# Replanning the order of a threshold-attention kernel: planned scatter and split distances, and new draws

## The chip, the cores and the metric

One core of one Trainium2 chip runs the kernel. The engines are PE (matmuls), DVE, ACT and POOL (element-wise work), and SP, which here only issues DMAs. The metric is the device time of one execution in microseconds (us); smaller is better.

## What is computed

Attention over 96 heads (batch 8, 12 heads, 512 rows, 64 columns), in which only weights above a threshold of 0.1 are kept and then normalised again:

```
scores  = einsum('bhqd,bhkd->bhqk', Q, K) / sqrt(64)
weights = exp(scores - max);  weights /= sum(weights) + 1e-10
weights = where(weights > 0.1, weights, 0)
weights /= sum(weights) + 1e-10
out     = einsum('bhqk,bhkd->bhqd', weights, V)
```

With these random inputs few rows have a weight above 0.1. A row that has none is zero in the output, and a row with exactly one has that key's V row as its output.

## The kernel before

**The idea.** The kernel writes zeros over the whole output, finds the rows that can have a weight above the threshold with cheap arithmetic, recomputes those few rows exactly, fetches the V row of the key that was found, and scatters it into the output. A dense path behind a check at the end is there for inputs with many such rows; it isn't taken here.

**The work.** Two heads make a pair (48 pairs, `hp`), four heads a quad (24 quads, `hq`), eight heads a group (12 groups, `j`, 0 to 11).

For each quad the *main run* does the following. SP loads K (`k_sb`), POOL loads Q as 16-bit floats (`q_sb`, L221). PE transposes K (`ktr`, L333), ACT or DVE copies it out (`kt`, L317 or L319), and POOL casts each pair's half to 16 bits (`kf`, L321). POOL or DVE reorders Q (`qm`, L321 or L319), PE transposes it (`qtr`, L370), and DVE or ACT copies it out (`qt`). For each pair PE then makes four blocks of scores (`qk`, L386), ACT or DVE takes an exponential of each (`exp`, L394 or L396, a 128x1024 block each), PE sums and compares each block's keys with 32 matmuls a pair (`d`, L405), and DVE reduces that to one number a row (`dred`, L413).

For each group, eight units of work after its last exponentials (`LAG`), a chain of small steps follows:

- `flags` (L417, POOL or DVE) marks the rows that may exceed the threshold; `size` and `rank` (L429, L435, L437, PE) check sizes and number the flagged rows; `key` (L441, DVE) and `oh` (L445, DVE) turn the numbers into a one-hot; `idx` (L456, PE), `half` and `idxev` (L466, DVE) make the row indices.
- `gather` (L471, POOL) is an indirect DMA that fetches the flagged rows of Q; `split` (L479, POOL or DVE) puts them into `qb`; `xtr` (L486, PE), `xev` (copy to `xq`), `xqk` (L500, PE) and `xexp` (L507, ACT) recompute their scores and weights exactly.
- `tv` (L513, POOL or DVE) and `found` (L518, DVE) find the key above the threshold; `vidx` (L525) makes its index; `fetch` (L536, POOL) is an indirect DMA that fetches the V row into `vsel`, which `vzero` (L532, POOL) has cleared; `scatter` (L542, POOL) is an indirect DMA that writes it to the output.

**What sets the order.** A planner in the kernel's Python (`Schedule`) lays the steps out before anything is built. Each step is added with the engines it may run on and for each a pair of numbers, (occupancy, latency): the engine is taken for the first, and whoever depends on the step may start when the second is over. A step also has the steps it depends on, a due place (`prio`), and the buffers it takes and gives back. The planner always takes the step that can start first, and among those within 0.06 the one with the smallest due place. `DRAWS` is a list of seeds: each moves a random share of the due places (2, 10 or 40 per cent) by up to 2.5 either way, one draw on top of the other. So every number in the planner acts on the whole order and on the choice between engines.

The steps are then emitted in the planned order, and `keep` ties each instruction behind the one that was emitted before it on its engine. Two kinds of instruction can still move when the program is built. K loads and zero writes on SP aren't kept. And an indirect DMA emits a register move of its own (the trace shows it on POOL's queue at L471, L536 and L542); `keep` ties the DMA to that move, and the move to nothing. So a gather, fetch or scatter can stand earlier in the built program than in the plan, while the steps that were emitted behind it stay behind it.

POOL executes in order: while a scatter at the head waits for its V rows, the steps behind it (kf, qm, flags, tv) wait too.

Of the kernel before, what the change touches and what calls it, by code (L numbers as in the profile page):

```python
# [11 lines left out]
class Schedule:  # L12
# [10 lines left out]
    def add(self, name, engs, deps, prio, fn, takes=(), gives=()):  # L23
        self.ids[name] = len(self.ops)
        self.ops.append((name, engs, list(deps), prio, fn, list(takes), list(gives)))

    def order(self, draws=()):

        ops, ids = self.ops, self.ids
        shift = [0.0] * len(ops)  # L30
        for draw in draws:
            rng = random.Random(draw)
            share = (0.02, 0.1, 0.4)[draw % 3]
            for i in range(len(ops)):
                if rng.random() < share:
                    shift[i] += rng.uniform(-2.5, 2.5)
        n = len(ops)
        succ = [[] for _ in range(n)]
        need = [0] * n
        ready_at = [0.0] * n  # L40
        for i, op in enumerate(ops):
            for d in op[2]:
                succ[ids[d]].append(i)
                need[i] += 1
        free_at = {}
        taken = {p: [] for p in self.bufs}
        given = {p: {} for p in self.bufs}
        users = {}
        for op in ops:
            for at in op[6]:  # L50
                users.setdefault(at, [0, 0.0])[0] += 1
        ready = {}

        def offer(i):
            for eng in ops[i][1]:
                ready.setdefault(eng, []).append(i)

        for i in range(n):
            if need[i] == 0:
                offer(i)  # L60
        out = []

        def start(i, eng):
            t = max(ready_at[i], free_at.get(eng, 0.0))
            want = {}
            for pool, _ in ops[i][5]:
                k = len(taken[pool]) + want.get(pool, 0)
                want[pool] = want.get(pool, 0) + 1
                if k >= self.bufs[pool]:
                    at = k - self.bufs[pool]  # L70
                    rel = given[pool].get(taken[pool][at]) if at < len(taken[pool]) else None
                    if rel is None:
                        return None
                    t = max(t, rel)
            return t

        while len(out) < n:
            best = None
            for eng, lst in ready.items():
                ts = [(start(i, eng), i) for i in lst]  # L80
                ts = [(t, i) for t, i in ts if t is not None]
                if not ts:
                    continue
                t0 = min(t for t, _ in ts)
                prio, t, i = min((ops[i][3] + shift[i], t, i) for t, i in ts if t <= t0 + 0.06)
                if best is None or (t, prio) < best[:2]:
                    best = (t, prio, i, eng)
            assert best is not None, "the schedule is stuck"
            t, _, i, eng = best
            name, engs, deps, prio, fn, takes, gives = ops[i]  # L90
            occ, lat = engs[eng]
            for other in engs:
                ready[other].remove(i)
            out.append((t, i, eng))
            free_at[eng] = t + occ
            for pool, key in takes:
                taken[pool].append(key)
            for pool, key in gives:
                left = users[pool, key]
                left[0] -= 1  # L100
                left[1] = max(left[1], t + lat)
                if left[0] == 0:
                    given[pool][key] = left[1]
            for j in succ[i]:
                ready_at[j] = max(ready_at[j], t + lat)
                need[j] -= 1
                if need[j] == 0:
                    offer(j)
        self.timeline = sorted(out)
        self.taken = taken  # L110
        self.makespan = max(t + ops[i][1][eng][1] for t, i, eng in out)
        return [(ops[i][4], eng) for t, i, eng in self.timeline]
# [3 lines left out]
def kernel(  # L116
# [68 lines left out]


    LAG, WARM = 8.0, 7
    DRAWS = (67013, 12429, 32834, 12225, 15210, 2031, 21369, 91932)

    consts = ctx.enter_context(tc.tile_pool(name="consts", bufs=1))  # L190
    kload = ctx.enter_context(tc.tile_pool(name="kload", bufs=6))
# [24 lines left out]
    def load_q(hq, parts=1):  # L216
# [15 lines left out]
        out=identity_f32[:], in_=identity_f32[:],  # L232
# [6 lines left out]
        out=group_f[:], in_=group_f[:], compare_op=ALU.is_ge, fill=-1.0,  # L239
# [3 lines left out]
        out=group_f[:], in_=group_f[:], compare_op=ALU.is_ge, fill=-1.0,  # L243
# [176 lines left out]
    def do_size(j, n, eng):  # L420
        if n == 0:
            rk = mpsum.tile([P, 3 * KEY], f32, name="sm", tag="sm")
            T["rk", j] = rk
        rk = T["rk", j]
        for which in range(2):
            sq = T["kq"[which] + "sq", 2 * j + n // 2]
            for r in range(R):
                at = (1 + which) * KEY + n * C2 + 2 * r
                keep(nc.tensor.matmul(rk[:, at:at + 2], lhsT=sq[:, n % 2, r * P:(r + 1) * P], rhs=heads[:],  # L429
                                      start=True, stop=True))  # L430
# [122 lines left out]
    def do_check(part, eng):  # L553
        if part == 0:
            keep(nc.vector.tensor_scalar(ok_all[:], keys[:], SLOTS + 0.5, None, op0=ALU.is_le))
            keep(nc.vector.tensor_reduce(ok_one[:, 0:1], ok_all[:], axis=AX.XY, op=ALU.min))
        else:
            okk = small.tile([P, NO], f32)
            keep(nc.vector.tensor_scalar(okk[:], kept[:], -20000.0, None, op0=ALU.is_ge))
            keep(nc.vector.tensor_reduce(ok_one[:, 1:2], okk[:], axis=AX.X, op=ALU.min))  # L560
            keep(nc.vector.tensor_reduce(oks[:], ok_one[:], axis=AX.X, op=ALU.min))
# [12 lines left out]
    for hq in range(NQ):  # L574
        u0 = 8 * hq
        j = hq // 2
# [62 lines left out]
        last = j == NO - 1  # L639

        def stage(name, engs, deps, fn, takes=(), gives=(), j=j, x=x):
            add((name, j), engs, deps, x, lambda e: fn(j, e), takes=takes, gives=gives)

        stage("flags", {"POOL": (0.25, 0.4), "DVE": (0.12, 0.3)}, [("dred", 4 * j + n) for n in range(4)] + ["casts"], do_flags)
        for n in range(4):
            add(("size", j, n), {"PE": (0.2, 0.23)},
                [("ksq", 2 * j + n // 2), ("qsq", 2 * j + n // 2)] + ([("flags", j)] if n == 0 else [("size", j, n - 1)]), x,
                lambda e, j=j, n=n: do_size(j, n, e), takes=[("sm", ("rk", j))] if n == 0 else [],
# [4 lines left out]
        stage("idx", {"PE": (0.5, 0.78)}, [("oh", j)], do_idx, takes=[("sm", ("ix", j))])  # L653
        stage("half", {"DVE": (0.08, 0.24), "ACT": (0.2, 0.36)}, [("idx", j)], do_half)
        stage("idxev", {"DVE": (0.13, 0.30)}, [("half", j)], do_idxev, gives=[("sm", ("ix", j))])
        stage("gather", {"POOL": (1.1, 4.2 if last else 5.5)}, [("idxev", j)], do_gather)
        stage("split", {"POOL": (0.4, 0.55), "DVE": (0.21, 0.37)}, [("gather", j), ("half", j)], do_split)
        stage("xtr", {"PE": (0.12, 0.42)}, [("split", j)], do_xtr, takes=[("sm", ("xp", j))])
        stage("xev", {"DVE": (0.2, 0.35), "ACT": (0.2, 0.36)}, [("xtr", j)], do_xev, gives=[("sm", ("xp", j))])
# [4 lines left out]
        stage("found", {"DVE": (0.80, 1.0)}, [("tv", j)], do_found)  # L664
        stage("vidx", {"POOL": (0.22, 0.36), "DVE": (0.12, 0.28)}, [("found", j)], do_vidx)
        stage("vzero", {"POOL": (0.12, 0.25)}, [("gather", j)], do_vzero)
        stage("fetch", {"POOL": (1.1, 4.2 if last else 7.0)}, [("vidx", j), ("vzero", j)], do_fetch)
        stage("scatter", {"POOL": (1.1, 3.0)}, [("fetch", j), ("z", 2 * j), ("z", 2 * j + 1)], do_scatter)
        if last:
            stage("check0", {"DVE": (1.0, 1.2)}, [("key", j)], lambda j, e: do_check(0, e))  # L670
            stage("check1", {"DVE": (0.4, 0.6)}, [("found", j), ("check0", j)], lambda j, e: do_check(1, e))
    for step, eng in sched.order(DRAWS):
        step(eng)
# [105 lines left out]
```

## Time and profile before

| what | us |
|---|---|
| median of 3 runs (lowest to highest) | 245.99 (245.85 to 246.08) |
| the profiled execution | 244.09 |
| its span, from first to last instruction | 242.4 |
| busy: PE, DVE, ACT, POOL | 201.0, 182.4, 159.3, 130.7 |
| scatters' waits on POOL for V rows (L542) | 20.5 in 10 waits |
| splits' waits on POOL for gathered Q rows (L479) | 3.1 in 2 waits |

The first three rows are three views of one thing: the span is what the trace covers, the profiled execution's time holds what lies around it, and the median is of executions without a profile. Busy times count an engine's instructions; an engine can be idle because it waits for another, and the waits by engine name whom. The granted clock is the share of its full speed that PE was allowed in a stretch of time. "Landing" is the time from a DMA's issue until its data is there: a median of 3.1 us for the gathers, 3.6 for the fetches.

### The profile page before, as it was taken

Reading aid. Unit: us, or ns where it says so; the run is one execution under the profiler, and the core shown is the slowest. Engines: PE = TensorE matmul, PEld = TensorE weight load, DVE = VectorE, ACT = ScalarE, POOL = GpSimd, SP = SyncE. Lnnn points to the kernel's source line nnn. Section 1 sums busy time; section 2 is a strip of 40 time slices with the busy share of each in tenths; the row PEclk is TensorE's granted clock in tenths of the full one; section 3 lists DMA queues with packets and bytes.
Section 4 is the critical chain, followed back from the end, with each engine's and each line's share of the span. In section 5 each row is a group of like instructions: output and inputs, shape, how many; then the busy total and the mean of one; then the engine's idle time right before and its main releaser. Section 6 shows DMA issues by size and latency. Waiting matters only on the chain.

```text
span 242.4 us, 7238 instructions
## 1 busy us (share of the span) xinstructions
PE 201.0 (83%) x2997; PEld 128.3 (53%) x2997; DVE 182.4 (75%) x313; ACT 159.3 (66%) x190; POOL 130.7 (54%) x214
## 2 busy tenths in 40 slices
PE   6596999999699499999699998999995978993510
PEld 2274567666456247766456766666754455672000
DVE  5669779989597388999668899989796587795220
ACT  2466698988478187899559869898785576860110
POOL 5528055376444766567746857728666228233441
PEclk9779799999979679999979999999998599996555
DMA  7999989999999957464752685555540000000000
GB/s 135 209 228 344 212 290 292 288 275 257 348 342 251 250 87 136 63 110 99 137 88 51 118 130 88 92 117 111 70 94 9 0 3 8 3 8 5 2 6 14
DMA packets 68021, 32.55 MB, mean 134 GB/s; under 512 B 52278, under 2 KB 64708, under 8 KB 67985
## 3 DMA queue, kind: packets, MB, share of 16 engines
q1 hardware_dynamic: 53088, 24.91, 37.9%
q0 software_dynamic: 13840, 6.88, 21.9%
q8 instruction: 24, 0.39, 0.7%
q10 hardware_dynamic: 1056, 0.26, 0.5%
q14 instruction: 13, 0.10, 0.1%
HBM read 25.95 MB, written 12.98 MB: 161 GB/s over the span
## 4 chain that ended last, share of the span: by engine, by line
PE 51%; POOL 14%; issue 11%; DVE 11%; DMA 6%; ACT 5%; POOLq 0%; ACTq 0%; DVEq 0%
PE sc L386 16%; PE sm L405 14%; PE sc L333 8%; DVE e L396 5%; PE sm L500 4%; DMA vsel<-in_V_dram,vidx 4%; PE smh L370 3%; POOL kf L321 3%; POOL qsel L471 3%; PE sm L429 3%; ACT e L394 3%; POOL out_dram L542 2%; DMA k_sb<-in_K_dram 2%; POOL qm L321 2%; PE sm L456 2%
## 5 line engine op out<-in xcount | busy, mean ns | idle before, releaser
L394 ACT ACTIVATE e<-sc 128x1024 bf16<-128x1024 f32 x130 | 128.0, 1024 | 39.7 <-PE sc L386 38.3
L386 PE MATMUL sc<-qt,kf 64*128 64x512 f16 x384 | 69.8, 406 | 13.4 <-POOL kf L321 7.2
L396 DVE TENSOR_SCALAR e<-sc 128x1024 int16<-128x1024 f32 x62 | 75.0, 1219 | 7.6 <-PE sc L386 7.2
L405 PEld LDWEIGHTS <-e 128*128 128x128 bf16 x1536 | 54.5, 101 | 24.8 <-issue 23.9
L405 PE MATMUL sm<-groups,e 128*128 128x64 bf16 x1536 | 63.8, 198 | 0.6 <-DVE idx L466 0.4
L321 POOL CAST kf<-kt 128x512 f16<-128x512 f32 x46 | 28.9, 644 | 35.9 <-DVE kt L319 16.9
L413 DVE TENSOR_REDUCE stat<-sm 128x8 f32<-128x512 f32 x48 | 32.8, 685 | 10.9 <-PE sm L405 10.6
L386 PEld LDWEIGHTS <-kf 64*128 64x128 f16 x384 | 17.5, 95 | 32.1 <-issue 16.6
L333 PE MATMUL sc<-identity_f,k_sb 128*128 128x128 f32 x192 | 31.9, 297 | 1.5 <-DMA k_sb<-in_K_dram 1.5
L321 POOL COPY qm<-q_sb 128x512 f16<-128x512 f16 x43 | 26.6, 634 | 1.8 <-DMA q_sb<-in_Q_dram 1.7
L333 PEld LDWEIGHTS sc<-identity_f,k_sb 128*128 128x128 f32 x192 | 22.2, 150 | 9.0 <-issue 4.2
L542 POOL DMA_INDIRECT out_dram<-vsel,idx x12 | 12.5, 1038 | 20.8 <-DMA vsel<-in_V_dram,vidx 20.5
L221 POOL DMA_DIRECT2D q_sb<-in_Q_dram x25 | 20.4, 815 | 4.6 <-POOL qm L321 1.5
L370 PE MATMUL smh<-identity_h,qm 128*128 128x128 f16 x192 | 16.1, 229 | 4.7 <-POOL qm L321 2.8
L319 DVE COPY kt<-sc 128x1024 f32<-128x1024 f32 (+1 forms) x13 | 15.3, 1179 | 5.8 <-PE sc L333 5.7
L507 ACT ACTIVATE xe<-sm 128x512 f32<-128x512 f32 x12 | 7.2, 597 | 19.0 <-PE sm L500 18.9
L317 ACT COPY kt<-sc 128x1024 f32<-128x1024 f32 (+1 forms) x12 | 11.7, 979 | 8.7 <-DVE kt L319 4.6
L471 POOL DMA_INDIRECT qsel<-in_Q_dram,idx x12 | 12.9, 1076 | 8.4 <-DVE idx L466 5.9
L370 PEld LDWEIGHTS <-qm 128*128 128x128 f16 x192 | 12.0, 101 | 9.7 <-issue 4.6
L536 POOL DMA_INDIRECT vsel<-in_V_dram,vidx x12 | 13.5, 1122 | 5.2 <-POOL vidx L525 3.3
L500 PE MATMUL sm<-kt,xq 128*32 128x512 f32 x96 | 15.6, 726 | 0.6 <-DVE xq L319 0.5
L353 DVE TENSOR_SCALAR ksq<-kf 128x1024 int16<-128x1024 int16 x24 | 11.4, 475 | 4.8 <-POOL kf L321 4.8
(84 smaller groups left out, 176.1 us busy)
## 6 DMA issues: line engine op xcount, KB each, us to landing
out_dram<-zero SPq DMA_DIRECT2D x24, 512.0 KB, 6.2
k_sb<-in_K_dram SPq DMA_DIRECT2D x94, 128.0 KB, 4.3
q_sb<-in_Q_dram POOLq DMA_DIRECT2D x23, 256.0 KB, 5.0
k_sb<-in_K_dram ACTq DMA_DIRECT2D x2, 128.0 KB, 4.2
q_sb<-in_Q_dram POOLq DMA_DIRECT2D x2, 128.0 KB, 5.3
qsel<-in_Q_dram,idx POOLq DMA_INDIRECT x12, 3.1
vsel<-in_V_dram,vidx POOLq DMA_INDIRECT x12, 3.6
out_dram<-vsel,idx POOLq DMA_INDIRECT x12, 2.6
```

Of the source, the lines that this page charges most:

```text
L221: keep(nc.gpsimd.dma_start(out=q_sb[:, part].rearrange("p h r d -> p h (r d)"), in_=Q4[hq][:, part]))
L321: keep(nc.gpsimd.tensor_copy(dst, src))
L333: keep(nc.tensor.matmul(T["ktr", hq][:, n, r * P:(r + 1) * P], lhsT=k_sb[:, r, :, :].rearrange("p h d -> p (h d)"), rhs=identity_f32[:], i ...
L370: keep(nc.tensor.matmul(T["qtr", hq][:, n, r * P:(r + 1) * P], lhsT=T["qm", hq][:, n, r].rearrange("p h d -> p (h d)"), rhs=identity_h[:], ...
L386: keep(nc.tensor.matmul(sc[:, h, :], lhsT=T["kf", hq][ps, n, c * P:(c + 1) * P], rhs=T["qt", hq][ps, n, :], start=True, stop=True))
L394: keep(nc.scalar.activation(e[:], sc[:], ACTF.Exp, scale=scale))
L396: keep(nc.vector.tensor_scalar(e[:].bitcast(i16), sc[:], BITS_A, BITS_B, op0=ALU.mult, op1=ALU.add))
L405: keep(nc.tensor.matmul(T["d", hp][:, j, :], lhsT=T["e", hp, c][:, h, qt * P:(qt + 1) * P], rhs=groups[:], start=(c == 0), stop=(c == R - 1)))
L413: keep(nc.vector.tensor_reduce(T["stat", j][:, n, :], T.pop(("d", hp))[:], axis=AX.X, op=ALU.max))
L471: keep(nc.gpsimd.indirect_dma_start(out=qsel_bufs[j % NS][:], out_offset=None, in_=Qr, in_offset=bass.IndirectOffsetOnAxis(ap=T["idx", j][ ...
L500: keep(nc.tensor.matmul(sc[sl, :], lhsT=xq[:, sl], rhs=T["kt", 2 * j + n // 2][:, n % 2, :], start=True, stop=True, tile_position=(0, n * ...
L542: i = nc.gpsimd.indirect_dma_start(out=Or, out_offset=bass.IndirectOffsetOnAxis(ap=T.pop(("idx", j))[:, 0:1], axis=0), in_=T.pop(("vsel", ...
```

## The change

Three things change in the planner, and nothing in the arithmetic.

- The latency of `fetch`, which is the least planned distance from a fetch to its scatter, goes from 7.0 to 16.0 (the last group: 4.2 to 4.4). That of `gather`, the least planned distance to its split, goes from 5.5 to 7.5 (the last group: 4.2 to 4.4).
- The list of draws is another and has twelve seeds instead of eight.
- The plan is handed on in the order in which the planner took the steps, instead of sorted by planned start.

```diff
-        self.timeline = sorted(out)
+        self.timeline = out
...
-    DRAWS = (67013, 12429, 32834, 12225, 15210, 2031, 21369, 91932)
+    DRAWS = (55125, 12429, 78892, 43664, 17346, 65358, 95610, 46971, 68712, 54930, 91140, 80100)
...
-        stage("gather", {"POOL": (1.1, 4.2 if last else 5.5)}, [("idxev", j)], do_gather)
+        stage("gather", {"POOL": (1.1, 4.4 if last else 7.5)}, [("idxev", j)], do_gather)
...
-        stage("fetch", {"POOL": (1.1, 4.2 if last else 7.0)}, [("vidx", j), ("vzero", j)], do_fetch)
+        stage("fetch", {"POOL": (1.1, 4.4 if last else 16.0)}, [("vidx", j), ("vzero", j)], do_fetch)
```

What the built program makes of it, by counting instructions: the work is the same, and some steps that may run on several engines change places.

| step | before: DVE, ACT, POOL | after: DVE, ACT, POOL |
|---|---|---|
| `exp` | 62, 130, - | 67, 125, - |
| `qmix` | 5, -, 43 | 12, -, 36 |
| `kev`, whole copies | 12, 11, - | 10, 13, - |
| `qev`, whole copies | 13, 10, - | 11, 12, - |
| `split` | 3, -, 9 | 5, -, 7 |
| `tv` | 4, -, 8 | 1, -, 11 |
| `vidx` | 0, -, 12 | 3, -, 9 |
| `flags` | 0, -, 12 | 1, -, 11 |

## The prediction

> **What bounds the kernel now.** I read the busy shares first: PE 201.0 of 242.4 us, DVE 182.4, ACT 159.3, POOL 130.7. PE is the bound and POOL is the idlest, so I looked for what stops PE, in the waits by engine. These are PE's waits for POOL's casts, flags and mixes, and POOL's largest wait (waiter, who is waited for, us in total, times, longest):
>
> ```profile
> PE sc L386 <- POOL kf L321: 7.2, 4, 3.8
> ...
> PE sm L435 <- POOL flags L417: 3.5, 2, 1.8
> ...
> PE smh L370 <- POOL qm L321: 2.8, 1, 2.8
> ...
> POOL out_dram L542 <- DMA vsel<-in_V_dram,vidx: 20.5, 10, 3.8
> ```
>
> PE waits for POOL, though POOL is idle half of the time. The last line says why: the scatter (L542) stands at the head of POOL's queue until its fetched V rows have landed, and the casts and flags behind it wait too. The timeline shows it at scatters 1 and 7 (start us, us; idle time before it and who ended it in brackets):
>
> ```profile
> 80.40 1.03 POOL L542 DMA_INDIRECT out_dram<-vsel,idx  x1 [3.79 <-DMA vsel<-in_V_dram,vidx]
> ...
> 82.11 0.61 PE L386 MATMUL sc<-qt,kf 64*128 64x512 f16 x2 [3.76 <-POOL kf L321]
> ```
>
> ```profile
> 185.84 1.04 POOL L542 DMA_INDIRECT out_dram<-vsel,idx  x1 [1.60 <-DMA vsel<-in_V_dram,vidx]
> ...
> 187.88 0.61 PE L370 MATMUL smh<-identity_h,qm 128*128 128x128 f16 x4 [2.78 <-POOL qm L321]
> ```
>
> Two more stops come behind scatter 0 (PE waits 1.82 for flags, until 65.50) and scatter 3 (2.25 for kf, until 120.57). Together 1.82 + 3.76 + 2.25 + 2.78 = 10.6 us. Each is then paid again, as the stretch table shows (us, then busy us of PE, PEld, DVE, ACT, POOL, granted clock, DMA share, GB/s):
>
> ```profile
> 78.00:81.00 3.00, 0.35 (x4) 0.11 (x1) 1.23 (x1) 0.89 (x1) 0.60 (x1) 0.92 1.07 288
> 81.00:84.00 3.00, 1.89 (x20) 1.09 (x20) 0.81 (x1) 1.02 (x1) 3.00 (x7) 0.50 0.99 231
> 84.00:87.00 3.00, 3.00 (x30) 1.77 (x28) 2.45 (x2) 1.75 (x2) 2.27 (x5) 0.50 0.89 170
> 87.00:90.00 3.00, 3.00 (x48) 1.78 (x49) 2.81 (x5) 2.66 (x4) 1.75 (x4) 0.94 0.51 64
> ```
>
> After the stop the granted clock is 0.50 for about 6.8 us, and half of that is lost: 3.4. In the same table the clock is halved for about 6.8 us after scatter 7 and 3.4 us after scatters 0 and 3. Lost: 1.7 + 3.4 + 1.7 + 3.4 = 10.2. **The four stops cost 20.8 us.**
>
> **When a scatter stops PE.** I counted, in the built order, the PE work between the exact scores of group j (L500) and the first matmul that needs what POOL does behind scatter j. Rates are the full-clock rows of the chain of waits: 1.04 us for 32 matmuls of L405, 0.54 for 4 of L386, 0.93 for 8 of L333, 0.55 for 8 of L370, 1.00 for the 8 of L500, 0.59 for the 8 of L456, 0.69 for 24 of L429. Behind scatter 7, for instance, qm is needed after 8 L456, 16 L386, 64 L405, 8 L333, 8 L370 and 32 L429: 0.59 + 2.16 + 2.08 + 0.93 + 0.55 + 0.9 = 7.2. I call it cover (us; the waited-for tile beside it).
>
> | scatter | 0 | 1 | 2 | 3 | 4 | 5 | 6 | 7 | 8 |
> |---|---|---|---|---|---|---|---|---|---|
> | cover before | 8.7 flags | 8.4 kf | 13.7 kf | 7.8 kf | 11.6 kf | 11.1 qb | 10.3 kf | 7.2 qm | 9.8 qb |
> | PE waited | 1.82 | 3.76 | - | 2.25 | - | - | - | 2.78 | - |
> | cover after | 9.0 flags | 9.8 qm | 9.7 flags | 9.8 flags | 10.4 kf | 10.6 qm | 7.7 kf | 10.0 kf | 7.8 flags |
>
> The four stops are the four smallest covers. On the other side stands the way from L500's exponential (L507) to the end of the scatter: the fetch starts 3.0 to 5.3 us later (4.5 is the middle), fetch to scatter takes 3.3 to 4.2 where nothing else stands between, but 5.9 and 6.3 at groups 0 and 1, scatter 1.04. With the operation behind it (flags 0.4, kf or qm 0.6) that is 9.5 to 10.2, and 11.9 to 13 at groups 0 and 1. PE needs 1.05 to 1.15 us for 1 us of counted work (8.05 for 7.8 at scatter 3; 10.06 for 8.7 at scatter 0; 51.4 for 46.0 from group 4 to 7), so a cover of 9.7 lasts 10.7.
>
> **Part by part.** *The scatter's planned distance (fetch 7.0 to 16.0).* The built order doesn't keep it: between fetch and scatter stand now, for groups 0 to 11, 2, 2, 1, 2, 1, 3, 0, 1, 1, 0, 1, 0 POOL operations, against 1, 1, 4, 1, 2, 5, 4, 1, 5, 0, 1, 0 before. The DMA is pinned only to its own register move, and that move is free. So POOL's 20.5 us of waits stay, about: I cost this at 0. What the larger number does is leave room behind the fetch in the plan, seen as cover.
>
> *Cover, from the table.* Removed: 20.8. Added: scatter 0, flags ready at 11.9, needed at 9.0 x 1.15 = 10.4: 1.5 and 1.7 of clock, 3.2. Scatter 6, ready at 4.5 + 3.4 + 1.04 + 0.6 = 9.5, needed at 7.7 x 1.05 = 8.1: 1.5 and 1.7, 3.2. Scatter 8, flags ready at 9.5, needed at 8.2: 1.3 and 1.7, 3.0. Scatter 1: qm ready between 10.2 (landing as in group 3) and 13.5 (as it was), needed at 10.8: between 0 and 6.1 with a long clock loss; I take 1.0, since the zero writes that crowd the DMA end near 79 us and fetch 1 moves 5 us of PE work later. Scatters 2, 3, 4, 5, 7: first operation ready 9.6 to 10.8, needed 10.7 to 11.6: 0, with 0 to 1 us to spare. Sum added 10.4.
>
> *Splits behind gathers (5.5 to 7.5).* PE work from the index matmul (L456) to the query transpose (L486) rises from 7.3 to 9.4 (10.8 in group 0) to 10.2 to 12.1 in groups 0 to 9. PE waited for qb only 1.21 and 2.23 us, in the last two groups. POOL's 1.96 before a split at 48.23 is hidden: PE ran. Nothing before the tail; above 0 only if DVE, which now does 5 splits of 12 in order, stood waiting for a gather (0 to 3.1, the median landing): 0.
>
> *Order drawn anew.* Counting the built rows: DVE gets 5 exponentials (L396, 1.22 each) and 7 query mixes (about 0.35), gives up 2 kt (1.22) and 2 qt (0.69) copies, with small ones net +6.4 us; ACT net -1.6; POOL -5.8. DVE is busy 26.5 of 30 us in the undisturbed 30 to 60. Cost between 0 (fits in the gaps) and 6.4 (all on the path); exponentials go to either engine, so I take half of what both gain, 2.4. Recording the plan as drawn instead of sorted leaves each engine's own order: 0; not below, since nothing is removed.
>
> *Tail.* Before, the last L405 ends at 217.57, 24.8 us before the end. The last flags now run on DVE right behind the last reduction instead of behind a scatter and a gather (218.31 to 219.58: -1.3), but a split and an xq copy come ahead of the keys (+0.8). The check (0.46 + 1.35) moves behind the one-hot, beside PE's index matmuls (-0.7). The last tv no longer stands behind scatter 10 (231.72 to 232.89 instead of 0.1: -1.1). Sum -2.3; between +1, if the tv of group 10, now behind scatter 9, comes late, and -3.
>
> **Sum.** -20.8 + 10.4 + 0 + 2.4 - 2.3 = -10.3, against the profiled execution's 244.09 (span 242.4): 233.8. The median of the runs, 245.99, is 1.9 above it: **235.7 us**.
>
> [...]
>
> **Rivals.**
> 1. *The short stops leave the clock alone.* A wait of 0.81 for kf at 203.0 was followed by a granted clock of 1.00; 1.82 was not. Mine lie between. Without 3 x 1.7: 230.6.
> 2. *DVE becomes the bound.* All 6.4 on the path instead of 2.4, and four slips of 0.5 at the thin covers: +6.0, 241.7. For it: DVE's 26.5 of 30. Against: PE is busier there (29.0).
> 3. *Slower: covers moved to where they all just fail.* The old order had 10 to 14 us at scatters 2, 4, 5, 6; the new one has 9.7 to 10.6 at 2, 3, 4, 5, 7. If fetch to scatter takes over 4.8 us there, all five stop PE for about 1 us and lose 1.7 of clock: 13.5, and 1 each at 6 and 8: 251. For it: 5.9 and 6.3 under full DMA. Against: 3.3 to 4.2 in the groups without zero writes. From four such stops on the gain is gone.
> 4. *It doesn't do what it says and nothing else matters:* the scatters stand as close as before, and the stops move without changing in sum: 246.
>
> **Chances.** Forecast (231.5 to 239) 0.42, rival 1 (228 to 231.5) 0.18, rival 2 (239 to 245.4) 0.15, rival 4 0.04, rival 3 (246.5 to 252) 0.21. A measurement can tell about 0.2% (0.5 us) from no change. Faster 0.75, same 0.04, slower 0.21. The range 228.5 to 248 leaves out most of rival 3 and the edge of rival 1; the likeliest case alone is 231.5 to 239.
>
> **What would show it.** Right: PE's waits for POOL's kf, qm and flags fall from 13.5 to about 6 us; the halved clock after scatters 1, 3 and 7 is gone, with stops left at 0, 6 and 8; POOL's wait for V rows stays near 20; the last L405 ends near 210 and the end follows within 22.5 us. Wrong: stops of over 1 us at scatters 2 to 5 or 7, fetch to scatter over 4.8 us, or PE waiting for DVE's and ACT's exponentials in a stretch without stops.

## The result, and the profile after

The changed kernel takes **233.91 us** (median of 4 runs, 233.74 to 235.06) against 245.92 for the kernel before in the same comparison (4 runs, 245.2 to 246.08): a ratio of 0.9527, interval 0.9491 to 0.9563. The profiled execution takes 233.86 us, its span is 232.0. The forecast was 235.7 in a range of 228.5 to 248. Some executions of a kernel are 1 or 2 per cent slower than its others: the times here are medians of all, the ratios with their intervals compare the faster ones alone, and the profiles of experiment 5's second kernel (237.18) and of experiment 7 (245.17) are of slower ones.

The page's first part, after (busy us, share of the span, instructions):

```profile
PE 195.5 (84%) x2997; PEld 126.3 (54%) x2997; DVE 186.8 (81%) x327; ACT 157.3 (68%) x186; POOL 125.7 (54%) x204
```

PE is busy 5.5 us less with the same 2997 matmuls; between group 0's L507 and the last L405 its clock is halved for 13.7 us instead of 20.5. DVE is busy 4.4 us more. The waits by engine, after (waiter, who is waited for, us in total, times, longest):

```profile
PE sm L486 <- DVE qb L479: 4.6, 2, 4.4
PE sc L386 <- DVE e L396: 3.6, 4, 1.9
...
PE smh L370 <- POOL qm L321: 1.2, 1, 1.2
PE sc L386 <- POOL kf L321: 1.1, 2, 0.7
...
PE sm L435 <- POOL flags L417: 0.2, 1, 0.2
```

```profile
POOL out_dram L542 <- DMA vsel<-in_V_dram,vidx: 18.7, 9, 3.7
```

PE's waits for POOL's casts, mixes and flags fell from 13.5 us to 2.5, although POOL waits at the scatters nearly as long as before (18.7 against 20.5). The largest wait, 4.4 for `qb`, is in the tail.

New is what stands at scatter 0. The timeline there, after:

```profile
61.70 0.20 PE L405 MATMUL sm<-groups,e 128*128 128x64 bf16 x1 [1.45 <-ACT e L394]
...
64.03 1.04 POOL L542 DMA_INDIRECT out_dram<-vsel,idx  x1 [3.36 <-DMA vsel<-in_V_dram,vidx]
...
65.38 0.63 POOL L321 CAST kf<-kt 128x512 f16<-128x512 f32 x1
...
66.04 0.81 DVE L353 TENSOR_SCALAR ksq<-kf 128x1024 int16<-128x1024 int16 x1 [3.36 <-POOL kf L321]
...
68.03 1.04 PE L386 MATMUL sc<-qt,kf 64*128 64x512 f16 x4 [1.92 <-DVE e L396]
```

PE names DVE's exponential as what it waited for, but the cause stands two steps back: the `kf` cast came late behind scatter 0, the square `ksq` (L353) that needs it stood at the head of DVE's queue for 3.36 us, and the exponentials behind it were late. The stretches around it (us, then busy us of PE, PEld, DVE, ACT, POOL, granted clock, DMA share, GB/s) show the clock:

```profile
63.00:66.00 3.00, 3.00 (x54) 1.73 (x50) 0.00 (x0) 2.11 (x3) 1.94 (x4) 0.50 1.02 289
66.00:69.00 3.00, 1.08 (x9) 0.25 (x6) 2.95 (x5) 0.42 (x1) 2.68 (x6) 0.50 0.68 231
69.00:72.00 3.00, 3.00 (x34) 2.94 (x33) 1.91 (x3) 1.02 (x1) 0.01 (x1) 0.50 1.00 253
```

DVE does nothing from 63 to 66, and PE's clock is halved for 10.2 us (62.9 to 73.1). The halving begins before PE waits for anything behind the scatter, and after the wait of 1.45 for ACT's exponential that ends at 61.70: not all of it belongs to scatter 0 (experiment 5). From 73.1 to the last L405 the clock is low only for 3.4 us, from 110.6.

**Where the time went.** PE work is counted at the prediction's rates, from one group's L500 to the next one's. A unit of it takes 1.10 to 1.17 us in stages 2-3, 4-5, 5-6 and 6-7 before the change, which have no stop. What a stage, from one L507 to the next, takes above 1.10:

| from group to group | 0-1 | 1-2 | 2-3 | 3-4 | 4-5 | 5-6 | 6-7 | 7-8 | 8-9 | sum |
|---|---|---|---|---|---|---|---|---|---|---|
| before | 3.7 | 6.2 | 0.1 | 3.4 | 0.2 | 0.9 | 0.3 | 4.6 | 2.3 | 21.8 |
| after | 6.8 | 1.9 | 0.2 | 2.0 | 2.4 | 1.2 | 1.0 | -0.3 | 2.0 | 17.3 |

4.5 us come from there. Another 2.3 come from the start: group 0's L507 begins at 53.6 us in both kernels, but PE has done 36.9 us of counted work by then instead of 34.8. The last L405 ends at 210.14 instead of 217.57, 7.4 sooner, and the end follows 21.8 us later instead of 24.8: 3.0.

### The profile page after: what moved, and what is told of

It is laid out like the page before. It is cut to its first block, busy times and chain, and to the rows that moved or that the text cites. A ratio compares the mean times of both kernels' runs of the same rounds, so it can differ in the third digit from the quotient of the medians.

```text
span 232.0 us, 7237 instructions
## 1 busy us (share of the span) xinstructions
PE 195.5 (84%) x2997; PEld 126.3 (54%) x2997; DVE 186.8 (81%) x327; ACT 157.3 (68%) x186; POOL 125.7 (54%) x204
## 4 chain that ended last, share of the span: by engine, by line
PE 48%; DVE 17%; DMA 11%; issue 8%; ACT 8%; POOL 6%; POOLq 0%; ACTq 0%; DVEq 0%
PE sm L405 15%; PE sc L386 14%; PE sc L333 8%; DMA vsel<-in_V_dram,vidx 8%; DVE e L396 7%; ACT e L394 5%; PE smh L370 3%; PE sm L429 3%; PE sm L500 3%; DVE stat L413 2%; DMA k_sb<-in_K_dram 2%; POOL out_dram L542 2%; DVE kt L319 2%; DVE ksq L353 2%; DMA qsel<-in_Q_dram,idx 1%
## 5 line engine op out<-in xcount | busy, mean ns | idle before, releaser
L394 ACT ACTIVATE e<-sc 128x1024 bf16<-128x1024 f32 x125 | 122.7, 1026 | 30.2 <-PE sc L386 27.3
L396 DVE TENSOR_SCALAR e<-sc 128x1024 int16<-128x1024 f32 x67 | 81.2, 1218 | 2.9 <-PE sc L386 1.7
L386 PE MATMUL sc<-qt,kf 64*128 64x512 f16 x384 | 67.4, 399 | 8.2 <-DVE e L396 3.6
L405 PEld LDWEIGHTS <-e 128*128 128x128 bf16 x1536 | 53.9, 100 | 25.5 <-issue 20.7
L405 PE MATMUL sm<-groups,e 128*128 128x64 bf16 x1536 | 63.3, 196 | 4.5 <-ACT e L394 1.8
L321 POOL COPY qm<-q_sb 128x512 f16<-128x512 f16 x36 | 22.8, 653 | 1.8 <-DMA q_sb<-in_Q_dram 1.6
L542 POOL DMA_INDIRECT out_dram<-vsel,idx x12 | 12.4, 1032 | 20.7 <-DMA vsel<-in_V_dram,vidx 18.7
L370 PE MATMUL smh<-identity_h,qm 128*128 128x128 f16 x192 | 15.5, 221 | 4.6 <-DVE qt L319 2.0
L317 ACT COPY kt<-sc 128x1024 f32<-128x1024 f32 x13 | 13.2, 1014 | 6.0 <-PE sc L333 4.8
L507 ACT ACTIVATE xe<-sm 128x512 f32<-128x512 f32 x12 | 7.2, 603 | 14.3 <-PE sm L500 14.3
L317 ACT COPY qt<-smh 128x1024 f16<-128x1024 f16 x12 | 12.2, 1013 | 6.8 <-PE smh L370 4.5
L319 DVE COPY kt<-sc 128x1024 f32<-128x1024 f32 (+1 forms) x12 | 13.5, 1132 | 3.9 <-PE sc L333 3.9
L353 DVE TENSOR_SCALAR ksq<-kf 128x1024 int16<-128x1024 int16 x24 | 13.8, 576 | 3.4 <-POOL kf L321 3.4
L370 PEld LDWEIGHTS <-qm 128*128 128x128 f16 x192 | 11.4, 98 | 8.4 <-DVE qm L319 3.4
```

Of the source, the lines that this page charges most:

```text
L317: keep(nc.scalar.copy(dst, src))
L319: keep(nc.vector.tensor_copy(dst, src))
L321: keep(nc.gpsimd.tensor_copy(dst, src))
L353: keep(nc.vector.tensor_scalar(sq[:].bitcast(i16), src[:].bitcast(i16), 0x7FFF, 2, op0=ALU.bitwise_and, op1=ALU.logical_shift_right))
L370: keep(nc.tensor.matmul(T["qtr", hq][:, n, r * P:(r + 1) * P], lhsT=T["qm", hq][:, n, r].rearrange("p h d -> p (h d)"), rhs=identity_h[:], ...
L386: keep(nc.tensor.matmul(sc[:, h, :], lhsT=T["kf", hq][ps, n, c * P:(c + 1) * P], rhs=T["qt", hq][ps, n, :], start=True, stop=True))
```

## The experiments

They ran on three chips, on which the kernel before took 247.04 (the first four), 247.29 (the next four) and 243.91 us (the last three). Ratios are to the kernel before on the same chip. My theory was that of the prediction: PE stops behind scatters and loses clock after them, and the change removes that. The rivals were that the stops merely move, that the gain is one of the latencies or of the draws alone, and that the clock is hidden.

**1. Hold the four stopping scatters at their planned places.** Scatters 0, 1, 3 and 7 of the kernel before are tied behind the POOL step that was emitted before them, so that they can't move ahead of it:

```diff
-        i = nc.gpsimd.indirect_dma_start(
+        with (tc.issue_after([x for x in nc.cur_bb.bb.instructions if x.engine == mybir.EngineType.Pool][-1])
+              if j in (0, 1, 3, 7) else ExitStack()): i = nc.gpsimd.indirect_dma_start(
```

> The kernel before, with the scatters of groups 0, 1, 3 and 7 alone held at their planned place (7 to 9 POOL operations behind their fetch instead of 1). These are the four that stop PE. Theory (cover): the four stops and their halved clock were 20.8 us and go; something else is late next, so 12 to 20 us come off: 226 to 234. Rival (the stops only uncover a limit that stands right behind, DVE and ACT): at most 5 off, 241 or more.

238.07 us (235.03 to 239.44), ratio 0.9684 (0.9492 to 0.9875): by the ratio 7.8 less than before, between the two, with a wide interval. POOL's timeline at scatter 1, in this kernel:

```profile
75.24 1.16 POOL L536 DMA_INDIRECT vsel<-in_V_dram,vidx  x1 [0.42 <-POOL vidx L525]
...
77.72 0.62 POOL L321 CAST kf<-kt 128x512 f16<-128x512 f32 x1
78.28 0.61 POOL L321 COPY qm<-q_sb 128x512 f16<-128x512 f16 x1
...
83.61 1.07 POOL L542 DMA_INDIRECT out_dram<-vsel,idx  x1 [0.18 <-issue]
```

Casts and mixes now go ahead of the scatter, which waits for nothing when its turn comes. All four stops are gone, but well under half of the counted 20.8 us went with them. The way from group 0's L507 to group 9's takes 147.75 us instead of 155.50, 7.8 less. Stages 1-2, 3-4 and 7-8 are 4.8, 3.2 and 2.1 shorter; stage 0-1 isn't, since PE now waits 1.07 there for DVE's reduction and 0.60 for `qb`, and the clock is at half from 67.5 to 71.0. Stage 7-8 has a new wait in its place, again with 3.4 us at half clock:

```profile
183.57 0.43 PE L486 MATMUL sm<-identity_f,qb 128*128 128x128 f32 x1 [1.18 <-DVE qt L319]
```

So the stops are a cause, and removing all four doesn't bring what they were counted at.

**2. Hold the other five.** The edit of experiment 1 with another list:

```diff
-              if j in (0, 1, 3, 7) else ExitStack()): i = nc.gpsimd.indirect_dma_start(
+              if j in (2, 4, 5, 6, 8) else ExitStack()): i = nc.gpsimd.indirect_dma_start(
```

> The kernel before, with the scatters of groups 2, 4, 5, 6 and 8 alone held at their planned place. None of these stops PE. Theory: POOL waits less (2.9 of its 20.5 us of waits at scatters go) and the time does not move: 244 to 248. Rival (the distance of scatters itself is worth time, or holding a DMA in place is): about half of what holding all would bring, 236 to 242.

247.05 us (243.74 to 249.69): no change, as the theory says. The stops behind scatters 1, 3 and 7 stay (3.46, 2.25 and 2.51). The edit by itself brings nothing; only where PE was stopped does it count.

**3. Hold scatters 0 to 8 in the changed kernel.** In the changed kernel:

```diff
-        i = nc.gpsimd.indirect_dma_start(
+        with (tc.issue_after([x for x in nc.cur_bb.bb.instructions if x.engine == mybir.EngineType.Pool][-1])
+              if j < 9 else ExitStack()): i = nc.gpsimd.indirect_dma_start(
```

> The changed kernel, with the scatters of groups 0 to 8 held at their planned place, 10 to 19 POOL operations behind their fetch: the planned distance is really kept. Theory: what is left behind scatters 0, 1, 6 and 8 (about 10 us against the undisturbed pace, 6.7 of it at scatter 0 through DVE's ksq) goes, 7 to 10 off: 224 to 227. Rival (DVE at 81% or the pace of the exponentials binds by now): 3 off at most, 231 to 234.

240.94 us (238.74 to 242.68), ratio 0.9889 (0.9779 to 0.9999). Both sides missed: it is slower than the changed kernel itself (0.9527 and, in experiment 5, 0.9512). POOL's waits for V rows fall to 5.0 us and the first two stages are shorter (16.70 and 15.64 us against 21.58 and 16.95, with no halved clock in them), but later PE waits for ACT's and DVE's exponentials (1.28, 2.09 and 1.41 us), and the clock falls for 10.2 us before group 9. In the changed kernel's profile it doesn't fall there, in experiment 5's of the same kernel it does for 3.4 us. The stretches before group 9, in the changed kernel and then here:

```profile
195.00:198.00 3.00, 2.45 (x40) 1.88 (x36) 1.59 (x5) 1.87 (x3) 1.81 (x3) 1.00 0.08 12
198.00:201.00 3.00, 2.25 (x48) 1.43 (x48) 3.00 (x6) 2.50 (x4) 2.58 (x6) 1.00 0.05 13
```

```profile
195.00:198.00 3.00, 2.70 (x29) 1.54 (x26) 0.82 (x3) 1.09 (x3) 1.96 (x2) 1.00 0.08 13
198.00:201.00 3.00, 1.98 (x45) 1.51 (x46) 2.80 (x6) 2.81 (x3) 1.32 (x3) 0.71 0.05 12
201.00:204.00 3.00, 3.00 (x35) 1.66 (x33) 2.67 (x3) 2.05 (x2) 0.47 (x2) 0.50 0.00 0
```

PE is idle for 1.30 of these first six us in the one and 1.32 in the other, and only the second loses its clock, from 199.2 to 209.5.

**4. The new latencies with the old draws.** In the kernel before:

```diff
-        stage("gather", {"POOL": (1.1, 4.2 if last else 5.5)}, [("idxev", j)], do_gather)
+        stage("gather", {"POOL": (1.1, 4.4 if last else 7.5)}, [("idxev", j)], do_gather)
...
-        stage("fetch", {"POOL": (1.1, 4.2 if last else 7.0)}, [("vidx", j), ("vzero", j)], do_fetch)
+        stage("fetch", {"POOL": (1.1, 4.4 if last else 16.0)}, [("vidx", j), ("vzero", j)], do_fetch)
```

> The kernel before with the two latencies changed (7.5 and 16.0; 4.4 in the last group) and nothing else; the old eight draws, the sorted plan. Cover counted in its built order, groups 0 to 8: 8.7 flags, 11.3, 11.4, 7.4 kf, 9.8, 11.3, 8.6 kf, 9.6, 9.4. Theory: stops at scatters 0 and 3 stay (3.5 and 3.7 with the clock), one of about 1 at scatter 6: 8 instead of 20.8, so 233, give or take 3 for the tail and the pace. Rival (the new draws bring the gain): 241 to 250.

243.88 us (242.39 to 245.17), ratio 0.9956 (0.9899 to 1.0013). The theory missed, and the time is in the rival's range; its reason, that the draws bring the gain, is for experiment 6. The stops behind scatters shrink as meant (1.30 for flags, 0.76 for `kf`, none larger), but in this order PE waits for exponentials instead:

```profile
PE sc L386 <- DVE e L396: 4.4, 7, 1.0
PE sc L386 <- ACT e L394: 4.0, 10, 0.7
```

The last L405 ends at 218.90, no sooner than before.

**5. The changed kernel again, and its scatters 0 and 1 held.** First without an edit, as a yardstick on this chip; then, in the changed kernel:

```diff
-        i = nc.gpsimd.indirect_dma_start(
+        with (tc.issue_after([x for x in nc.cur_bb.bb.instructions if x.engine == mybir.EngineType.Pool][-1])
+              if j < 2 else ExitStack()): i = nc.gpsimd.indirect_dma_start(
```

> The changed kernel itself, unchanged, on the same chip as the runs beside it, so that its variants are compared with it there. Both theories: 0.95 to 0.96 of the kernel before.

> The changed kernel with the scatters of groups 0 and 1 alone held at their planned place. In the run that held the scatters of groups 0 to 8 the stretches from group 0 to 2 came 6 us sooner, and the last 40 us later by as much, with a halved clock that the changed kernel did not have there. Theory: the early gain is real and is kept, 4 to 6 us below the changed kernel beside it. Rival (what is saved early is waited for later, by the exponentials): within 1.5 of it.

The first: 235.27 us (233.12 to 238.89), 0.9512 (0.9454 to 0.9569), as on the other chip. The second: 235.45 us (233.04 to 238.71), 0.9516 (0.9457 to 0.9575), no difference. Stage 0-1 does become shorter, 18.03 us against 21.36, so scatter 0 made it longer by about 3.3. What is left there comes without the scatter: the wait for ACT's exponential stays, and 3.4 us of halved clock (63.2 to 66.6) with it:

```profile
63.23 0.23 PE L405 MATMUL sm<-groups,e 128*128 128x64 bf16 x1 [1.46 <-ACT e L394]
```

But 2-3 takes 18.29 us (15.55 in the first), with a wait of 2.67 for an exponential at 98.76, and before group 9 the clock is low for 10.2 us instead of 3.4 (199.8 to 210.0). Here too the rival held: what is gained at scatters 0 and 1 is given back. Where it is given back rests on one execution, 1.7 us above the median.

**6. The new draws with the old latencies.** In the kernel before:

```diff
-    DRAWS = (67013, 12429, 32834, 12225, 15210, 2031, 21369, 91932)
+    DRAWS = (55125, 12429, 78892, 43664, 17346, 65358, 95610, 46971, 68712, 54930, 91140, 80100)
```

> The kernel before with the twelve new draws and nothing else (latencies 5.5 and 7.0, sorted). Cover in its built order, groups 0 to 8: 9.0 flags, 10.6, 10.5, 10.8, 10.7, 12.9, 9.0 kf, 8.9 qm, 9.7 at the least. Theory: a stop behind scatter 0 like that of the changed kernel, small ones at 6 and 8; 8 to 14 below the kernel before. Rival (the new latencies are what brings the gain, the draws are noise): at most 4 below.

250.4 us (248.07 to 253.74), ratio 1.0126 (1.0054 to 1.0197): slower than before, and the theory missed. So the draws by themselves don't bring the gain. PE's stops are other ones: 1.13 for flags at 66.71, 2.73 for an exponential at 69.79, 2.02 for a `qb` behind a gather at 140.29, and 2.71 for `qm` behind scatter 8, with 6.8 us of halved clock at the first two together and at each of the others.

**7. The changed kernel with the old fetch latency.**

```diff
-        stage("fetch", {"POOL": (1.1, 4.4 if last else 16.0)}, [("vidx", j), ("vzero", j)], do_fetch)
+        stage("fetch", {"POOL": (1.1, 4.2 if last else 7.0)}, [("vidx", j), ("vzero", j)], do_fetch)
```

> The changed kernel with the fetch's latency back at 7.0 (4.2 in the last group) and all else as changed. Cover as in the changed kernel up to group 5, then 8.0 kf at group 6 and 6.4 kf at group 8 (7.8 there in the changed kernel). Theory: one more stop, behind scatter 8, of 2 with a halved clock: 2 to 6 above the changed kernel beside it. Rival (the 16.0 does nothing, since scatters are not held there): within 1. Second rival (the 16.0 is the change): 6 or more above.

241.94 us (237.82 to 247.85), ratio 0.9706 (0.9611 to 0.9801) against the changed kernel's 0.9512: 6.7 above it by the medians, 4.8 by the ratios. So the 16.0 counts, but with runs this far apart the theory (2 to 6) and the second rival (6 or more) can't be told from each other. The order changes, and two large stops are back, both behind scatters (6 and 8), in this kernel's timeline of PE:

```profile
174.46 0.61 PE L386 MATMUL sc<-qt,kf 64*128 64x512 f16 x2 [2.77 <-POOL kf L321]
...
208.79 0.61 PE L386 MATMUL sc<-qt,kf 64*128 64x512 f16 x2 [3.00 <-POOL kf L321]
```

The covers are 8.0 and 6.4 us by the prediction's count. At scatter 6 flags and a load of Q (0.85) also stand ahead of `kf`, so the first counted need was met 10.3 us after L507.

**8. The tail alone.** In the kernel before, the last group's flags and `tv` go to DVE, and the first half of the check goes behind the last one-hot:

```diff
-        e = nc.gpsimd if eng == "POOL" else nc.vector
+        e = nc.gpsimd if eng == "POOL" and j < NO - 1 else nc.vector
...
-        T["oh", j] = oh
+        T["oh", j] = oh; (j == NO - 1 and do_check(0, "late"))
...
-        if part == 0:
+        if eng == "late":
```

(the first in `do_flags` and `do_tv`; in `do_check`, `else` becomes `elif part == 1`, so that the planned first half emits nothing)

> The kernel before with the last group's steps ordered as the changed kernel's plan has them, nothing else changed: the last flags (L416) and the last tv (L511) on DVE, the first half of the check behind the last one-hot. Theory (the tail is a part of the gain by itself): the end comes 2 to 3 us sooner after the last L405 than 24.8, time 2 to 3.5 below the kernel before. Rival (the end of the tail is set by the last scatters and transfers): within 1 us of the kernel before.

242.47 us (239.13 to 245.49), ratio 0.9915 (0.9866 to 0.9964): by the ratio 2.1 us. In the profiled execution (240.99) the last L405 ends at 217.23 and the end follows 22.1 us later instead of 24.8. So the tail's gain stands by itself. The last `tv` in the kernel before and here:

```profile
231.78 1.04 POOL L542 DMA_INDIRECT out_dram<-vsel,idx  x1 [2.04 <-DMA vsel<-in_V_dram,vidx]
232.89 0.24 POOL L513 TENSOR_SCALAR tv<-sum 128x1 f32<-128x1 f32 x1
```

```profile
229.80 0.15 DVE L513 TENSOR_SCALAR tv<-sum 128x1 f32<-128x1 f32 x1 [2.99 <-ACT xe L507]
229.93 1.05 POOL L542 DMA_INDIRECT out_dram<-vsel,idx  x1 [2.13 <-DMA vsel<-in_V_dram,vidx]
```

It no longer stands behind scatter 10.

**9. Fill two stops with matmuls of zeros.** In the kernel before, so that PE isn't idle while it waits; the results are overwritten.

```diff
         sc = spsum.tile([P, 2, S], f32, name="sc", tag="sc")
+        [keep(nc.tensor.matmul(sc[:, 0, :], lhsT=warm[:, 0:P], rhs=warm[:], start=True, stop=True))
+         for _ in range({16: 17, 26: 10}.get(hp, 0) if c == 0 else 0)]
```

> The kernel before with matmuls of zeros added, whose results are overwritten: 17 of 128x512 ahead of the first scores of pair 16, 10 ahead of those of pair 26, which fill the PE stops behind scatters 1 (3.76) and 3 (2.25). The stops' own time stays, only PE's idleness goes. Theory (idleness lets the clock down, and the clock is a cost of its own): the halved stretches 80.5 to 87.4 and 121.5 to 124.9 are at full clock, 5.1 us gained (3.4 + 1.7), 3 to 6 below the kernel before. Rival (the halved clock is hidden behind the other engines, or comes at another place instead): within 1.5 us of the kernel before, or slower by what the added matmuls take.

242.36 us (240.98 to 243.91), ratio 0.9945 (0.9911 to 0.9979): 1.3 us less, within what the rival allowed, not what the theory expected. The stretches at stop 1, before and then here:

```profile
80.00:84.00 4.00, 1.89 (x20) 1.09 (x20) 0.81 (x1) 1.02 (x1) 3.60 (x7) 0.57 1.01 250
84.00:88.00 4.00, 4.00 (x37) 2.14 (x36) 3.29 (x4) 2.41 (x3) 2.33 (x6) 0.58 0.97 165
```

```profile
80.00:84.00 4.00, 4.00 (x34) 1.84 (x32) 1.14 (x2) 0.72 (x1) 3.42 (x7) 1.00 0.99 223
84.00:88.00 4.00, 3.40 (x55) 1.99 (x53) 3.98 (x5) 3.58 (x5) 3.23 (x7) 1.00 0.82 121
```

With PE busy the halved clock is gone at both stops (at the second the granted clock is 1.00 from 120 to 126, where it was 0.75 and 0.68): at these two it was PE's idleness that the halved clock followed. But behind stop 1 it hid another bound. At full clock DVE is busy for 3.98 of the next 4 us and ACT for 3.58, and PE is idle for 0.60. The stage 1-2 is 1.13 us shorter (1.7, if one adds the 0.6 by which the filling ran past `kf`), not 3.4; the stage 3-4 is 1.49 shorter of the counted 1.7. These are rough: stage 0-1, which the filling doesn't touch, is 0.8 longer in this profile.

**10. Hold the four scatters, and the tail.** The edits of 1 and 8 together, in the kernel before, with its old latencies and old draws:

```diff
-        i = nc.gpsimd.indirect_dma_start(
+        with (tc.issue_after([x for x in nc.cur_bb.bb.instructions if x.engine == mybir.EngineType.Pool][-1])
+              if j in (0, 1, 3, 7) else ExitStack()): i = nc.gpsimd.indirect_dma_start(
...
-        T["oh", j] = oh
+        T["oh", j] = oh; (j == NO - 1 and do_check(0, "late"))
```

> The kernel before with scatters 0, 1, 3 and 7 held at their planned places and the tail's three steps ordered as in the changed kernel: old latencies, old draws. Theory (the whole gain is the waits behind those scatters and the tail): 11 to 13 below the kernel before, the time of the changed kernel. Rival (the tail's gain does not add to the other): 8 to 10 below.

231.06 us (229.68 to 236.46, 6 runs), ratio 0.9447 (0.9387 to 0.9507): 12.9 less by the medians, 13.5 by the ratio, at the upper end of what the theory says or just above. In the profiled execution the last L405 ends at 206.50, and POOL waits 11.7 us at scatters. The interval overlaps that of the changed kernel (0.9491 to 0.9563; 0.9454 to 0.9569 on the second chip), so "as fast" is shown and "faster" is not. It is more than the two parts tried alone (7.8 and 2.1); the first of these is known to within 4.7 only, so the runs don't show whether the parts simply add. Stages 0-1, 1-2, 3-4 and 7-8 are 11.4 us shorter in all, against 10.0 in experiment 1. Where PE stopped for 1.82 us behind scatter 0, it still stops:

```profile
65.16 0.33 PE L486 MATMUL sm<-identity_f,qb 128*128 128x128 f32 x1 [1.00 <-POOL qb L479]
```

and the clock is at half for about 3.4 us after it.

**What follows from them together.** Taking away the waits behind scatters 0, 1, 3 and 7 and reordering the tail is enough for a gain as large as the change's (10), and each part counts by itself (1, 8). The changed kernel has both, and it also loses in other stages, so its gain is a balance and not these two parts alone. That the changed planner got rid of them isn't a matter of one number: the latencies alone bring between nothing and 1 per cent (4), the draws alone lose (6), and the draws need this fetch latency (7). Handing the plan on unsorted, and the gather's 7.5, weren't tried by themselves. Real distance between fetch and scatter, which the change names and the built program doesn't keep, brings nothing further (3, 5).

## Why the prediction was right, point by point

The mechanism was right: PE stopped behind four scatters. The stops behind scatters 3 and 7 went, the one behind 1 shrank from 3.76 to 1.22, the halved clock behind all three went, and the stop behind scatter 0 changed in kind. The sum was right too: -10.3 in the profiled execution, against 233.86 - 244.09 = -10.2 (-10.4 in the span). But several of its terms were not, and that they offset each other to 0.1 us is luck. The forecast's remaining error of 1.8 us is the 1.9 that I added for the median: before the change the profiled execution lay 1.9 under the median, after it 0.05 (233.86 and 233.91). The measured sizes in the table are the stages' costs above, whatever in a stage made them, and add up to the span's change.

| term | predicted | measured |
|---|---|---|
| four stops removed | -20.8 | -18.0 (3.7, 6.2, 3.4, 4.6) |
| scatter 0 after | 3.2 | 6.8 (3.3 of it by holding) |
| scatter 1 after | 1.0 | 1.9 |
| scatter 6 after, less what stage 6-7 already cost | 3.2 | 1.0 - 0.3 |
| scatter 8 after, less what stage 8-9 already cost | 3.0 | 2.0 - 2.3 |
| redraw: the other stages, less what they already cost | 2.4 | 4.4 (5.6 - 1.2) |
| start, to group 0 | 0 | -2.3 |
| from group 9 to the last L405 (the remainder) | 0 | -0.6 |
| tail | -2.3 | -3.0 |
| sum | -10.3 | -10.4 |

- **The four stops** were sized too high. Their stages cost 18.0 above the pace, not 20.8, and holding the four scatters took only 10.0 (experiment 1) and 11.4 us (experiment 10) of that away: other waits take part of their place (1.07 and 0.60, or 1.00, in group 0, and 1.18 in stage 7-8). The halved clock behind the stops was counted as lost in full. Filling two stops measured what the clock alone costs: about 1.7 of 3.4 behind scatter 1 and 1.5 of 1.7 behind scatter 3. With the clock back, DVE and ACT (busy 3.98 and 3.58 of the next 4 us) are the limit behind the longer stop.
- **Scatter 0** was the step that failed in its reason. I counted only PE's needs of what POOL does behind the scatter, found flags, and said 1.5 us of wait. PE had no wait for flags. The late `kf` stopped DVE, in order, at `ksq`, and that reached PE as 1.92 us of waiting for an exponential, after 1.45 for another at 61.70; the clock was low for 10.2 us, not 3.4. Cover has to be counted for every engine that reads what POOL makes. Holding scatters 0 and 1 shortened the stage by 3.3 us (21.36 to 18.03), which is close to the 3.2 forecast, by another way and so by luck. The rest of the 6.8, with 3.4 us of the halved clock, comes with the wait of 1.45, which the redraw brought: with the new draws alone (experiment 6) it is there too, 1.46 at 62.30.
- **Scatter 1**: a wait of 1.22 for `qm` inside the bounds of 0 and 6.1, next to the 1.0 taken, but not for the reason given. The DMA engines were still full (share 1.15 from 84 to 87) and fetch to scatter took 6.00 us, so `qm` was ready 12.6 us after L507, late in the range of 10.2 to 13.5. PE got to it late too, after 11.4 us instead of 10.8, and its clock stayed at 1.00.
- **Scatters 6 and 8** were sized too high (and stage 8-9 already cost 2.3 before, which no term held): 0.69 of wait at 6, and 0.22 for flags and 0.41 for `kf` at 8 (I said 1.5 and 1.3), with a granted clock of 1.00 behind both. L507 to the end of scatter 6 took 8.42 us, not 8.9, and the clock was the first rival's: short waits left it alone. That is one execution: in experiment 5's of the same kernel the clock is at half from 201.9 to 205.3, after a wait of 0.41 for `kf` behind scatter 8. The clock was left alone as well by waits of 1.22 at 87.8 and 1.39 (for DVE's `qm`) at 130.0. That term, 3 x 1.7, was wrong at scatters 6 and 8, and too small at 0.
- **Scatters 2, 3, 4, 5 and 7**: no wait of PE for POOL, as forecast; the stop of 1.39 at 130.0 is one for DVE. The sign that I named against the forecast, stops of over 1 us there, came only in that one, and not from a scatter. The third rival's condition, fetch to scatter over 4.8, was not met: 3.3 to 4.3.
- **The scatter's planned distance costs 0**: right; POOL's waits are 18.7 of 20.5, and the value of the number is in the plan (experiments 3 and 7).
- **Splits**: no stop behind a gather before the tail: right. In the tail the 4.42 us wait for `qb`, split on DVE, is longer than the two before (1.21 and 2.23), and I hadn't named it; it is inside the tail's measured sum.
- **Redraw**: I took 2.4 of 6.4. DVE got 4.4 busier, ACT 2.0 less, and the stages without a scatter stop cost 5.6, 4.4 more than before, with waits of 0.75 and 0.90 for exponentials, 1.39 for `qm`, and 3.4 us of halved clock at 110.6. With what stage 0-1 costs beside its scatter (about 3.3) that is more than the second rival's 6.4. The engine load and the clock aren't separated in it.
- **The start's 2.3** was in no term; I compared the plans only from group 0's L507 on. Before, PE waits 1.02, 0.74 and 0.52 for DVE's exponentials from 22 to 25.3, and its clock is at half from 25.9 to 29.3; after, the waits there are 0.39 and 0.44, and the clock stays at 1.00.
- **The other signs** came as named: the halved clock behind scatters 1, 3 and 7 is gone (the 3.4 us from 110.6 follow a wait of 0.75 for an exponential), the last L405 ends at 210.14 (near 210), the end follows within 22.5 us (21.8). PE's waits for POOL fell further than forecast, to 2.5 for 6. One sign against the forecast came as well: PE waits for exponentials in stretches without a scatter stop (0.75 and 0.90, and 1.45 ahead of scatter 0).
- **Tail**: -3.0 for -2.3; alone -2.7 by the profile, -2.1 (-3.3 to -0.9) by the ratio. The three steps that I named are enough for it; that each is worth what I gave it wasn't tried.

## What to carry to other kernels

When an in-order engine waits at the head of its queue, list every reader of what stands behind it, on every engine, and compare the work that each has left with the wait; the largest shortfall gives a first estimate of the price (with the clock, the four stops were put at 20.8 us here, and their stages cost 18.0), and the engine that reports the wait may be two steps from its cause, as at scatter 0, where PE waited 1.92 us for an exponential and the late step was a `kf` cast. A planner's latency is worth what it does to the whole order: test it with the old order's seeds and the new ones, since here neither the latencies nor the draws alone made the kernel faster by more than 1 per cent, and a hold on four instructions with three moved steps did as much as both. After removing a stop, don't count the slow clock behind it in full (of 3.4 us counted behind scatter 1, about 1.7 came back); look at which engine is busy next, and hold or fill a stop to measure what it is worth.

## What the runs showed of the hardware that I had not expected

- The same idle time of PE (1.30 and 1.32 of six us) was followed by a granted clock of 1.00 in one kernel and by 10.2 us at half in another, and single waits of 1.22 and 1.39 in the changed kernel were followed by a granted clock of 1.00. A wait for the same exponential was followed by 3.4 us at half clock in experiment 5 (1.46 us) and by none in experiment 3 (1.48).
- Up to the tail, the halved stretches of all thirteen profiles last 3.4, 6.8 or 10.2 us, and within a profile their edges stand whole multiples of 3.41 us apart (before: 66.9, 70.3, 80.5, 87.4, 121.5, 124.9, 186.4 and 193.2). So in these profiles the clock changed only at such edges. Cut at them, the profiles of before and after have 105 whole stretches of 3.41 us at full clock from 15 us to the last L405. Of the 95 with at most 0.90 us of idle PE none was followed by half clock, of the five with 1.07 to 1.57 us two were, and the five with 1.80 us or more all were. What decides in between, the runs don't show.
- Waits of 1.82, 2.25 and 2.78 us before the change were already followed by a halved clock for 3.4 to 6.8 us, and with the stops of 3.76 and 2.25 us filled in experiment 9 the granted clock was 1.00 behind both.
- A halved clock was half free here: in experiment 9 taking 6.8 us at half clock away shortened the stage by 1.1 to 1.7 us, where 3.4 had been counted.
